# Planning TensorE's order together with the other engines in a two-layer hybrid attention trunk

## The chip, the cores and the metric

The kernel runs on one core of one Trainium2 chip. A core has a matrix engine (TensorE, PE in the profile, its weight loads PEld), a vector engine (VectorE, DVE), a scalar engine (ScalarE, ACT), a general engine (GpSimd, POOL) and a sync engine (SyncE, SP), which here only issues transfers (DMAs). Each engine works through its own list of instructions in order and waits at semaphores where one of them needs what another engine makes. The metric is device time in microseconds (us) of one execution; lower is better.

## The reference

The input `x` is 1024 tokens by 1024 features, in float32. Two layers follow each other, each `x + W_out(mixer(RMSNorm(x)) * silu(gate))`, with 16 heads of 64.

```python
def fox_mixer(h, w_in, b_f, q_g, k_g):          # layer 1
    proj = h @ w_in                              # q, k, v, gate (1024 each), 16 forget logits
    q = rms_norm(q, q_g); k = rms_norm(k, k_g)   # per head
    c = cumsum(log_sigmoid(f_logit + b_f), axis=1)
    o = softmax(q k^T / 8 + c_q - c_k, causal) v # in blocks of 128 queries
    return o, gate

def dsw_mixer(h, cos, sin, w_in, q_g, k_g):     # layer 2
    proj = h @ w_in                              # 3 groups of q, k, v (9216) and gate (1024)
    for g, (window, dilation) in enumerate(((128, 1), (512, 4), (2048, 16))):
        o[g], lse[g] = dilated_window_attention(rotary(rms_norm(q[g])), rotary(rms_norm(k[g])), v[g], window, dilation)
    return softmax(lse over g) * o summed over g, gate
```

## The kernel before, in words

**Tiling.** The 1024 tokens are eight tiles of 128, the 1024 features eight slices of 128. Float32 operands of the large products are split into a high and a low float16 half: `xh`, `xl` for the activations, `w[:, 0]`, `w[:, 1]` for the weights. `project` (line 678, matmuls on line 683) makes one token tile times up to 384 columns in 8 x 3 = 24 matmuls (high by high, high by low, low by high for each slice) into one bank of PSUM, the accumulator memory, called `pj`. The pool `ps_pj` has three such banks, `ps_s` three for scores and small things (tag `s`), `ps_o` two for attention outputs (tag `o`).

**Stages.** `gates(0, ...)` projects the gate of layer 1 in three parts of columns; during its first part each token tile is normalised and split just ahead of its projection: `x_ready` calls `row_factor` (ACT and DVE make the tile's factor `dg`), `spread_factor` (line 933, two small matmuls into `nb`) and `split_xt` (lines 964 to 967, DVE, ACT, POOL). Eight blocks of two heads (`hp`) of forgetting attention follow: eight projections each, `heads_tile` and `heads_pair` (norms, a float16 pair `hl`), a transposing DMA into `qk_t` (line 823), `scores` (line 843, tile `s`), the exponentials, a transposing DMA into `ptt` (line 891) and the products with the values, `pv` (lines 898 to 900, tile `o`). Results go to `y_d` in DRAM and come back through `turn_y` and `transpose_rows` (line 717, tile `pt`); those of the last head pair through `turn_last`. The output projection is `project_t` (line 707) in three parts; `grown`, `factors` (line 1219, tile `so`) and `take` normalise and split for layer 2 (`xl` on line 1236). Layer 2 has the same gates, then 24 blocks (eight head pairs by three dilations, `dsw_pair`, outputs `ob`), and its own `project_t`.

**Weights.** A block of weights is loaded two blocks ahead into `raw`. `bound` (lines 617 to 623) takes its norms into `vm`, `scale` (`spread_sums`, line 590, a small matmul `ws` or into the spare columns of a running `pj`) makes a power of two, `split` (lines 648 to 653) the two halves. These calls are spread by a slot clock, `Flow`: `project` and `project_t` tick it, 32 ticks a block, and `flow.at(slot, fn)` puts work into the source at a later tick. `scale` of the next block is at tick 8.

**What sets the order.** Source order is what the Python loops and `Flow` give. TensorE keeps it: `manual_schedule` pins it (lines 423 and 424). The order of the other four engines is written out by a planner. `step_graph` finds what each instruction must follow, `latest_starts` when it is due, `plan_engines` (line 294) plays the program through with a duration for each instruction (`lasts`) and lists the others' instructions by due time among those ready, with 150 ns of slack (`SLACK`) on each hand-over between engines. `order_engines` then ties each engine's list together. In that play TensorE takes `pe[at]`, the next in source order, and waits for it. A DMA on SP is held until the last TensorE instruction ahead of it in the source has begun.

Of the kernel before, what the change touches and what calls it, by code (L numbers as in the profile page):

```python
# [103 lines left out]


BYTES = {"float32": 4, "float16": 2, "bfloat16": 2, "int32": 4, "float32r": 4}
OTHERS = ("DVE", "Activation", "Pool", "SP")
OVERLAP = {"PE": 0, "DVE": 80, "Activation": 95, "Pool": 42}
SIGNAL = {"PE": 70, "DVE": 33, "Activation": 40, "Pool": 80, "SP": 27}
DRAIN = 200  # L110
SLACK = 150


class Access:
# [160 lines left out]
def latest_starts(steps, deps, need):  # L275


    n, t = len(steps), 0.0
    late = [0.0] * n
    for k, x in enumerate(steps):  # L280
        late[k] = t if x.eng == "PE" else t + 30000.0
        t += x.ns if x.eng == "PE" else 0.0
    for k in range(n - 1, -1, -1):
        e = steps[k].eng
        for d in deps[k] | need[k]:
            x = steps[d]
            if x.eng == "PE":
                continue
            took = 1900 + x.moved() / x.rate() if x.eng == "SP" else x.ns
            late[d] = min(late[d], late[k] - took - (SIGNAL[e] if x.eng != e else 0))  # L290
    return late


def plan_engines(steps, deps, need, after, slots):


    n = len(steps)
    late = latest_starts(steps, deps, need)
    succ, starts, fills = [[] for _ in range(n)], [[] for _ in range(n)], [[] for _ in range(n)]
    left = [len(d) for d in deps]  # L300
    for k in range(n):
        for d in deps[k]:
            succ[d].append(k)
    for a, b in set(after):
        if steps[a].eng != "PE":
            starts[a].append(b)
            left[b] += 1
    for bufs, rows in slots:
        queue = [f for f, _ in rows[bufs:]][::-1]
        for f in queue:  # L310
            left[f] += 1
        for _, us in rows:
            slot = [len(us), 0.0, queue]
            for u in us:
                fills[u].append(slot)
    pe = [k for k in range(n) if steps[k].eng == "PE"]
    gate, c = [], -1
    for x in steps:
        c += x.eng == "PE"
        gate.append(c)  # L320
    ready, end, begun = [0.0] * n, [0.0] * n, [-1.0] * len(pe)
    held, pe_ready = {}, set()
    soon, now = ({e: [] for e in OTHERS} for _ in range(2))
    free = dict.fromkeys(("PE",) + OTHERS, 0.0)
    out = {e: [] for e in OTHERS}
    pool_end = lock_end = dma_end = 0.0
    at = 0

    def open_up(k):
        left[k] -= 1  # L330
        if left[k]:
            return
        e = steps[k].eng
        if e == "PE":
            pe_ready.add(k)
        elif e == "SP" and gate[k] >= 0 and begun[gate[k]] < 0:
            held.setdefault(gate[k], []).append(k)
        else:
            if e == "SP" and gate[k] >= 0:
                ready[k] = max(ready[k], begun[gate[k]])  # L340
            heapq.heappush(soon[e], (ready[k], late[k], k))

    for k in range(n):
        left[k] += 1
        open_up(k)
    for _ in range(n):
        best = None
        for e in free:
            if e == "PE":
                if at == len(pe) or pe[at] not in pe_ready:  # L350
                    continue
                t = max(free[e], ready[pe[at]])
            elif now[e]:
                t = free[e]
            elif soon[e]:
                t = max(free[e], soon[e][0][0])
            else:
                continue
            if best is None or t < best[0]:
                best = (t, e)  # L360
        t, e = best
        if e == "PE":
            k, begun[at] = pe[at], t
            for j in held.pop(at, ()):
                ready[j] = max(ready[j], t)
                heapq.heappush(soon["SP"], (ready[j], late[j], j))
            at += 1
        else:
            while soon[e] and soon[e][0][0] <= t:
                _, p, k = heapq.heappop(soon[e])  # L370
                heapq.heappush(now[e], (p, k))
            k = heapq.heappop(now[e])[1]
            out[e].append(steps[k].ins)
        x, s = steps[k], t
        if e == "SP":
            dma_end = max(dma_end, t + 400) + x.moved() / x.rate()
            free[e], end[k] = t + x.ns, dma_end + 1500
        else:
            if x.lock:
                s = max(t, pool_end - 190)  # L380
                lock_end = s + x.ns
            elif e == "Pool":
                s = max(t, lock_end - 150)
                pool_end = s + x.ns
            end[k] = s + x.ns
            free[e] = end[k] - OVERLAP[e]
        tail = DRAIN if e == "PE" else 0
        for slot in fills[k]:
            slot[0] -= 1
            slot[1] = max(slot[1], end[k] + tail)  # L390
            if not slot[0] and slot[2]:
                j = slot[2].pop()
                ready[j] = max(ready[j], slot[1] + SIGNAL[steps[j].eng] + SLACK)
                open_up(j)
        for j in starts[k]:
            ready[j] = max(ready[j], t)
            open_up(j)
        for j in succ[k]:
            q = steps[j].eng
            if q != e:  # L400
                ready[j] = max(ready[j], end[k] + tail + SIGNAL[q] + SLACK)
            elif e not in ("PE", "SP"):
                ready[j] = max(ready[j], end[k])
            elif e == "SP":
                ready[j] = max(ready[j], end[k] + SIGNAL[q] + SLACK)
            open_up(j)
    return out
# [12 lines left out]
@with_exitstack  # L420
def trunk(ctx, tc, ins, out, cfg):
    nc = tc.nc
    if cfg["pin"]:
        ctx.enter_context(tc.manual_schedule(engines={mybir.EngineType.PE}))
    x, pos = ins["x"], ins["pos"]
    norm_g, gains, b_f = ins["norm_g"], ins["gains"], ins["b_f"]
    w_fox, w_dsw = ins["w_fox"], ins["w_dsw"]
# [425 lines left out]
    def v_tile(t2):  # L853
        vt = lay([P, NT, 2, 129], F16, name="vt", tag="vt")
        nc.scalar.activation(vt[:, :, :, 128], t2.unsqueeze(2).broadcast_to([P, NT, 2]), AF.Copy, scale=VS)
        return vt
# [79 lines left out]
    def column_factor(t):  # L936

        sq = lay([P, D], F32, name="xsq", tag="ptt")
        nb = ps_s.tile([P, 512], F32, name="nb", tag="s")
        for h in range(2):  # L940
            nc.scalar.activation(sq[:, 512 * h : 512 * (h + 1)], xts[t, h], AF.Square)
            for k in range(4 * h, 4 * h + 4):
                nc.tensor.matmul(nb[:, :P], ones.bitcast(F32), sq[:, k * P : (k + 1) * P], start=(k == 0), stop=(k == KT - 1))
        v, a, y = (nb[:, i * P : (i + 1) * P] for i in (1, 2, 3))
        r = sm.tile([P, P], F32, name="dg", tag="dg", bufs=2)
        nc.vector.tensor_scalar(v, nb[:, :P], 1.0 / D, EPS, ALU.mult, ALU.add)
        nc.scalar.activation(r, v, AF.Ln)
        nc.scalar.activation(r, r, AF.Exp, scale=-0.5)
        nc.scalar.activation(a, r, AF.Square)
        c = sm.tile([P, P], F32, name="cf", tag="dg", bufs=2)  # L950
        nc.vector.tensor_copy(c, v)
        nc.vector.scalar_tensor_tensor(a, a, -0.5, c, ALU.mult, ALU.mult)
        nc.vector.scalar_tensor_tensor(y, a, 1.5, r, ALU.add, ALU.mult)
        return y
# [23 lines left out]
    nb = column_factor(0)  # L978
# [9 lines left out]
    nb = column_factor(1)  # L988
# [165 lines left out]
    for hp in range(NHP):  # L1154
# [11 lines left out]
        vt = v_tile(w.t2)  # L1166
        for t in range(NT):
            ps = project(w, tile_cols(0, t))
# [12 lines left out]
            if hp == NHP - 1:  # L1181

                a = max(flow.now + 1, s0 + cfg["due"][t] - 4 * NT + cfg["lpf"] + 9)
# [210 lines left out]
    for ci, (hp, g) in enumerate(order):  # L1394
# [5 lines left out]
        vt = v_tile(w.t2)  # L1400
        qks = [None]
        for t in range(NT):
            if ci == NHP - 1:
                reload_x(t)
            ps = project(w, tile_cols(g, t))
# [19 lines left out]
            else:  # L1425
                cmb = {}
# [30 lines left out]
    layer["cm"].__exit__(None, None, None)  # L1457


CFG = dict(pin=1, bc=((1, 0, 26), (1, 1, 28), (0, 0, 38), (0, 1, 46)), wpool=3, rbufs=8, ps=0, pv=100, ph_=100, ph=1, wbufs=8, pl=3, um=3, lpf=8, lsd=((16, 16), (16, 14), (14, 11)), ty2=((0, 4), (1, 5)), hb=2, ub=2, qb=1, nb=3, fox=(((0, 0, 2, 2), (2, 4)), ((0, 0), (4, 4))), due=(29, 33, 39, 45, 35, 41, 49, 57), l1=dict(ga=7, ptt=4, ph=3, p=4, qk_t=6, vt=3, gsl=3), l2=dict(ga=4, cmb=3, ptt=3, ph=3, p=2, qk_t=3, og=3, vt=3, gsl=3, par=1), wload=(18, 20, 22, 24), wbound=(0, 1, 3, 4), wscale=8, wsplit=(10, 16, 22, 12))  # L1460


def host_layout(inputs):
# [49 lines left out]
```

## Time and profile before

| | us |
|---|---|
| runs | 1745.38, 1737.65, 1745.68 |
| median | 1745.38 |
| the profiled execution, its own time | 1739.07 |
| its span, first to last instruction | 1737.3 |
| TensorE busy | 1628.6 |
| VectorE busy | 1244.4 |
| ScalarE busy | 1076.8 |
| GpSimd busy | 858.4 |

The profile is of one execution. Busy time is the union of an engine's instructions; TensorE's ends are modelled, so that its busy time is not time at its peak. A wait is idle time of an engine just before an instruction, put down to what released it last. The clock is the share of full speed that TensorE was granted. DMA share is the mean busy share of the core's 16 DMA engines.

### The profile page before, as it was taken

How to read it: one execution, taken by the hardware profiler on the slowest of the kernel's cores; microseconds unless marked ns; L12 is line 12 of the kernel's file. 1: busy time of each engine (PE TensorE's matmuls, PEld its weight loads, DVE VectorE, ACT ScalarE, POOL GpSimd, SP SyncE). 2: the span in 40 equal slices, each digit the busy share in tenths (PEclk: the TensorE clock that was granted, in tenths of full speed). 3: DMA queues.
4: the chain of work that ended last, by engine and by line, in shares of the span. 5: the costliest groups of instructions: out<-in, count | busy, mean ns of one | idle time of the engine just before them, and what ended most of it. 6: DMA issues, size and time to landing. Idle time of an engine off the chain costs nothing.

```text
span 1737.3 us, 37952 instructions
## 1 busy us (share of the span) xinstructions
PE 1628.6 (94%) x13342; PEld 1052.0 (61%) x13342; DVE 1244.4 (72%) x3906; ACT 1076.8 (62%) x2790; POOL 858.4 (49%) x1019
## 2 busy tenths in 40 slices
PE   5799999999989687999999999999999999999999
PEld 3465666666656333666666666666666666666544
DVE  6686777776767538767767788777877778778751
ACT  5564767767767346656666677666666666666630
POOL 3211556555555233115555556566665766657420
PEclk9899999999999899999999999999999999999999
DMA  6334899999998768425877899887678777978852
GB/s 206 106 121 110 191 199 192 198 198 204 211 190 198 195 187 245 125 94 125 161 158 137 156 186 194 167 173 157 149 180 168 172 156 155 193 156 163 192 174 103
DMA packets 658767, 292.86 MB, mean 169 GB/s; under 512 B 510208, under 2 KB 622848, under 8 KB 658576
## 3 DMA queue, kind: packets, MB, share of 16 engines
q1 hardware_dynamic: 658576, 290.44, 74.0%
q8 instruction: 104, 1.70, 0.4%
q14 instruction: 87, 0.71, 0.1%
HBM read 124.35 MB, written 41.22 MB: 95 GB/s over the span
## 4 chain that ended last, share of the span: by engine, by line
PE 76%; DVE 9%; DMA 8%; issue 3%; ACT 2%; SPq 1%; POOL 1%; DVEq 0%; ACTq 0%; POOLq 0%
PE pj L683 58%; PE pj L707 6%; PE s L843 6%; DMA qk_t<-hl 3%; DVE w L649 1%; DVE p L1083 1%; DMA raw<-in_w_fox 1%; DMA ptt<-ph 1%; PE ob L900 1%; PE ob L898 1%; PE ob L899 1%; DMA yt<-y_d 1%; PE pt L717 1%; DVE hl L819 1%; PE o L900 1%
## 5 line engine op out<-in xcount | busy, mean ns | idle before, releaser
L683 PE MATMUL pj<-w,xh 128*128 128x384 f16 (+2 forms) x4864 | 1179.9, 326 | 0.5 <-DVE vt L782 0.3
L683 PE MATMUL pj<-w,xl 128*128 128x384 f16 (+2 forms) x2432 | 792.7, 326 | 11.9 <-DVE xl L1236 11.9
L683 PEld LDWEIGHTS <-xh 128*128 128x128 f16 x4864 | 470.8, 99 | 281.1 <-issue 10.6
L683 PEld LDWEIGHTS <-xl 128*128 128x128 f16 x2432 | 239.8, 99 | 168.5 <-DVE xl L1236 14.4
L890 POOL TENSOR_TENSOR ph<-p,ph 128x512 f16<-128x512 f32 (+3 forms) x176 | 170.7, 990 | 162.8 <-issue 91.0
L1314 POOL TENSOR_TENSOR ph<-p,ph 128x768 f16<-128x768 f32 (+2 forms) x96 | 155.0, 1615 | 117.2 <-ACT ph L1313 112.1
L818 POOL TENSOR_TENSOR hl<-u,hl 128x512 f16<-128x512 f32 x128 | 158.2, 1236 | 90.3 <-ACT hl L817 89.4
L649 DVE SCALAR_TENSOR_TENSOR w<-raw,ws_f,w 128x768 f16<-128x768 f32 (+2 forms) x133 | 170.3, 1285 | 7.2 <-ACT w L648 6.7
L843 PE MATMUL s<-qk_t 128*128 128x128 f16 (+1 forms) x1504 | 159.2, 247 | 17.1 <-DMA qk_t<-hl 17.1
L707 PE MATMUL pj<-xh,w 128*128 128x512 f16 x512 | 160.5, 383 | 1.5 <-DVE xr L1198 1.5
L771 DVE TENSOR_TENSOR u<-pj,gr 128x256 f32<-128x256 f32 x256 | 107.3, 419 | 68.3 <-PE pj L683 66.1
L884 ACT ACTIVATE p<-p,acc 128x512 f32<-128x512 f32 (+2 forms) x192 | 110.6, 608 | 72.8 <-DVE acc L1083 69.1
L776 ACT ACTIVATE sq<-pj 128x256 f32<-128x256 f32 x256 | 96.6, 377 | 86.7 <-DVE u L771 85.0
L843 PEld LDWEIGHTS <-qk_t 128*128 128x128 f16 x1504 | 113.1, 98 | 31.4 <-DMA qk_t<-hl 18.9
L648 ACT ACTIVATE w<-raw,ws_f 128x768 f16<-128x768 f32 (+2 forms) x133 | 119.1, 912 | 15.5 <-DVE ws_f L631 11.7
L1309 ACT ACTIVATE p<-p,og 128x128 f32<-128x128 f32 (+1 forms) x256 | 105.1, 441 | 36.7 <-DVE og L1308 36.3
L707 PEld LDWEIGHTS <-w 128*128 128x128 f16 x768 | 74.6, 99 | 85.3 <-issue 5.3
L898 PEld LDWEIGHTS <-ptt 128*128 128x128 f16 x1136 | 106.1, 98 | 23.6 <-DMA ptt<-ph 11.7
L803 POOL TENSOR_TENSOR ra<-u,cs 128x128 f32<-128x128 f32 x96 | 44.8, 466 | 138.0 <-DVE u L771 135.2
L899 PEld LDWEIGHTS <-ptt 128*128 128x128 f16 x1136 | 105.5, 97 | 11.7
L651 POOL TENSOR_SCALAR raw<-raw,ws_f 128x768 f32<-128x768 f32 (+2 forms) x43 | 38.7, 900 | 149.1 <-DVE ws_f L634 53.7
L617 ACT ACTIVATE jk<-raw 128x768 f16<-128x768 f32 (+2 forms) x88 | 72.2, 820 | 60.0 <-DMA raw<-in_w_dsw 32.1
(212 smaller groups left out, 2911.3 us busy)
## 6 DMA issues: line engine op xcount, KB each, us to landing
raw<-in_w_dsw SPq DMA_DIRECT2D x96, 384.0 KB, 4.1
raw<-in_w_fox SPq DMA_DIRECT2D x32, 384.0 KB, 3.8
og_d<-og SPq DMA_DIRECT2D x64, 132.0 KB, 2.8
cmb<-og_d SPq DMA_DIRECT2D x64, 132.0 KB, 3.1
bc<-c_d SPq DMA_DIRECT2D x32, 256.0 KB, 3.8
gs_d<-ge SPq DMA_DIRECT2D x32, 192.0 KB, 2.1
xt<-in_xt SPq DMA_DIRECT2D x16, 256.0 KB, 4.6
gsf<-gs_d SPq DMA_DIRECT2D x64, 64.0 KB, 2.6
```

Source lines behind the costliest of these rows:

```text
L648: nc.scalar.activation(w[:, 0, :, :n], raw, AF.Copy, scale=self.sw)
L649: nc.vector.scalar_tensor_tensor(w[:, 1, :, :n], raw, self.sw, w[:, 0, :, :n], ALU.mult, ALU.subtract)
L683: nc.tensor.matmul(ps[:, :n], a[:, k, cols], w.slab(k, j), start=(k == 0 and i == 0), stop=(k == KT - 1 and i == 2))
L707: nc.tensor.matmul(ps[m], w.slab(k, j)[:, m * P : (m + 1) * P], a[:, k, 512 * b : 512 * (b + 1)], start=(k == 0 and x == 0), stop=(k == KT ...
L771: nc.vector.tensor_mul(u[:, t % 2].rearrange("p (a b) d -> p a b d", a=2), ps[:, : 4 * HD].rearrange("p (a b d) -> p a b d", a=2, b=2), gr ...
L818: nc.gpsimd.tensor_sub(hl[:, :, :4, 1], u, hl[:, :, :4, 0])
L843: nc.tensor.matmul(s[:, c0 : c0 + cnt * P].rearrange("p (c s) -> p c s", c=cnt), qk[:, i, blk], kk[:, j : j + cnt, e], start=(h == 0), sto ...
L884: nc.scalar.activation(p, p, AF.Exp, bias=acc, scale=-1.0)
L890: (nc.gpsimd if pool_l else nc.vector).tensor_sub(ph[:, e, 1, cols], p, ph[:, e, 0, cols])
L898: nc.tensor.matmul(o[:, e, :], hi, vt[:, j, e, HD:], start=(b == 0), stop=False, skip_group_check=True)
L899: nc.tensor.matmul(o[:, e, :HD], hi, vt[:, j, e, :HD], start=False, stop=False, skip_group_check=True)
L1314: nc.gpsimd.tensor_sub(ph[:, 1], st["p"], ph[:, 0])
```

## The change

TensorE is no longer pinned. In the planner it becomes an engine like the others: its instructions wait in `soon` until they are ready and then in `now`, from which the first in source order is taken, where the others take the one that is due first. A hand-over to TensorE carries a slack of 400 ns (`PE_SLACK`) where the others keep 150. The tiles of one tag (a bank of PSUM among them) still begin in source order, which now is an edge of the graph for TensorE too. A DMA on SP is held until as many TensorE instructions have been issued as stand ahead of it in the source. The list made for TensorE is tied together like the others'. No instruction is added, removed or altered.

```diff
-OTHERS = ("DVE", "Activation", "Pool", "SP")
+ENGINES = ("PE", "DVE", "Activation", "Pool", "SP")
+PE_SLACK = 400
...
     for a, b in set(after):
-        if steps[a].eng != "PE":
-            starts[a].append(b)
-            left[b] += 1
+        starts[a].append(b)
+        left[b] += 1
...
+    margin = {e: PE_SLACK if e == "PE" else SLACK for e in ENGINES}
...
-        if e == "PE":
-            pe_ready.add(k)
-        elif e == "SP" and gate[k] >= 0 and begun[gate[k]] < 0:
+        if e == "SP" and gate[k] > len(out["PE"]):
             held.setdefault(gate[k], []).append(k)
         else:
-            if e == "SP" and gate[k] >= 0:
-                ready[k] = max(ready[k], begun[gate[k]])
-            heapq.heappush(soon[e], (ready[k], late[k], k))
+            heapq.heappush(soon[e], (ready[k], k if e == "PE" else late[k], k))
...
-            if e == "PE":
-                if at == len(pe) or pe[at] not in pe_ready:
-                    continue
-                t = max(free[e], ready[pe[at]])
-            elif now[e]:
+            if now[e]:
                 t = free[e]
...
+        while soon[e] and soon[e][0][0] <= t:
+            _, p, k = heapq.heappop(soon[e])
+            heapq.heappush(now[e], (p, k))
+        k = heapq.heappop(now[e])[1]
+        out[e].append(steps[k].ins)
         if e == "PE":
-            k, begun[at] = pe[at], t
-            for j in held.pop(at, ()):
-                ready[j] = max(ready[j], t)
-                heapq.heappush(soon["SP"], (ready[j], late[j], j))
-            at += 1
-        else:
-            while soon[e] and soon[e][0][0] <= t:
-                _, p, k = heapq.heappop(soon[e])
-                heapq.heappush(now[e], (p, k))
-            k = heapq.heappop(now[e])[1]
-            out[e].append(steps[k].ins)
+            for j in held.pop(len(out[e]), ()):
+                heapq.heappush(soon["SP"], (max(ready[j], t), late[j], j))
...
             if q != e:
-                ready[j] = max(ready[j], end[k] + tail + SIGNAL[q] + SLACK)
+                ready[j] = max(ready[j], end[k] + tail + SIGNAL[q] + margin[q])
...
-    if cfg["pin"]:
-        ctx.enter_context(tc.manual_schedule(engines={mybir.EngineType.PE}))
```

More of the change, by code (lines that the diff above doesn't have):

```diff
@@ L315, in plan_engines @@
                 fills[u].append(slot)
-    pe = [k for k in range(n) if steps[k].eng == "PE"]
-    gate, c = [], -1
+    gate, c = [], 0
     for x in steps:
+        gate.append(c)
         c += x.eng == "PE"
[L320 to L325, printed above, removed]
+    ready, end = [0.0] * n, [0.0] * n
+    held = {}
+    soon, now = ({e: [] for e in ENGINES} for _ in range(2))
+    free = dict.fromkeys(ENGINES, 0.0)
+    out = {e: [] for e in ENGINES}
     pool_end = lock_end = dma_end = 0.0
-    at = 0
+    margin = {e: PE_SLACK if e == "PE" else SLACK for e in ENGINES}
     def open_up(k):
@@ L347, in plan_engines @@
         best = None
-        for e in free:
-            if e == "PE":
-                if at == len(pe) or pe[at] not in pe_ready:
-                    continue
-                t = max(free[e], ready[pe[at]])
-            elif now[e]:
+        for e in ENGINES:
+            if now[e]:
                 t = free[e]
@@ L392, in plan_engines @@
                 j = slot[2].pop()
-                ready[j] = max(ready[j], slot[1] + SIGNAL[steps[j].eng] + SLACK)
+                ready[j] = max(ready[j], slot[1] + SIGNAL[steps[j].eng] + margin[steps[j].eng])
                 open_up(j)
@@ L1457, in trunk @@
     layer["cm"].__exit__(None, None, None)
-CFG = dict(pin=1, bc=((1, 0, 26), (1, 1, 28), (0, 0, 38), (0, 1, 46)), wpool=3, rbufs=8, ps=0, pv=100, ph_=100, ph=1, wbufs=8, pl=3, um=3, lpf=8, lsd=((16, 16), (16, 14), (14, 11)), ty2=((0, 4), (1, 5)), hb=2, ub=2, qb=1, nb=3, fox=(((0, 0, 2, 2), (2, 4)), ((0, 0), (4, 4))), due=(29, 33, 39, 45, 35, 41, 49, 57), l1=dict(ga=7, ptt=4, ph=3, p=4, qk_t=6, vt=3, gsl=3), l2=dict(ga=4, cmb=3, ptt=3, ph=3, p=2, qk_t=3, og=3, vt=3, gsl=3, par=1), wload=(18, 20, 22, 24), wbound=(0, 1, 3, 4), wscale=8, wsplit=(10, 16, 22, 12))
+CFG = dict(bc=((1, 0, 26), (1, 1, 28), (0, 0, 38), (0, 1, 46)), wpool=3, rbufs=8, ps=0, pv=100, ph_=100, ph=1, wbufs=8, pl=3, um=3, lpf=8, lsd=((16, 16), (16, 14), (14, 11)), ty2=((0, 4), (1, 5)), hb=2, ub=2, qb=1, nb=3, fox=(((0, 0, 2, 2), (2, 4)), ((0, 0), (4, 4))), due=(29, 33, 39, 45, 35, 41, 49, 57), l1=dict(ga=7, ptt=4, ph=3, p=4, qk_t=6, vt=3, gsl=3), l2=dict(ga=4, cmb=3, ptt=3, ph=3, p=2, qk_t=3, og=3, vt=3, gsl=3, par=1), wload=(18, 20, 22, 24), wbound=(0, 1, 3, 4), wscale=8, wsplit=(10, 16, 22, 12))
 def host_layout(inputs):
```

## The prediction

> **What bounds the kernel now.** I read the page's busy line, its chain, then busy time by stage, and last TensorE's waits.
>
> ```profile
> span 1737.3 us, 37952 instructions
> PE 1628.6 (94%) x13342; PEld 1052.0 (61%) x13342; DVE 1244.4 (72%) x3906; ACT 1076.8 (62%) x2790; POOL 858.4 (49%) x1019
> PE 76%; DVE 9%; DMA 8%; issue 3%; ACT 2%; SPq 1%; POOL 1%; DVEq 0%; ACTq 0%; POOLq 0%
> ```
>
> TensorE (PE) is busy 94% of the span and 76% of the chain that ended last. 1737.3 - 1628.6 leaves 109 us in which it waits. The next view cuts the span into stages: first gate block (0:80), the rest of that layer's gates (80:160), forgetting attention (160:500), its end with the start of the output projection (500:590), that projection (590:640), passage to layer two (640:700), dilated attention (700:1600), end (two rows). Columns: stretch and length, busy us and count of PE, weight loads, DVE, ACT, POOL, then granted clock, DMA share, GB/s.
>
> ```profile
> 0.00:80.00 80.00, 48.66 (x257) 30.88 (x258) 55.58 (x128) 44.88 (x100) 28.08 (x33) 0.89 0.48 163
> 80.00:160.00 80.00, 77.63 (x533) 51.82 (x532) 59.89 (x168) 41.87 (x98) 10.64 (x8) 1.00 0.35 103
> 160.00:500.00 340.00, 321.09 (x3318) 226.15 (x3317) 248.25 (x853) 240.21 (x609) 192.24 (x187) 0.98 0.94 196
> 500.00:590.00 90.00, 75.05 (x772) 50.67 (x769) 55.00 (x166) 53.67 (x120) 38.27 (x37) 0.94 0.92 214
> 590.00:640.00 50.00, 37.31 (x168) 16.66 (x167) 24.39 (x67) 21.88 (x40) 12.12 (x10) 0.86 0.45 137
> 640.00:700.00 60.00, 45.26 (x222) 21.91 (x220) 49.02 (x58) 37.36 (x51) 19.77 (x14) 0.92 0.82 244
> 700.00:1600.00 900.00, 896.74 (x7307) 585.65 (x7306) 683.99 (x2281) 588.55 (x1659) 521.26 (x686) 1.00 0.75 159
> 1600.00:1680.00 80.00, 73.45 (x533) 44.20 (x532) 54.08 (x166) 44.97 (x113) 33.45 (x43) 0.98 0.79 190
> 1680.00:1738.00 58.00, 53.41 (x249) 24.08 (x246) 14.22 (x24) 3.43 (x4) 2.55 (x2) 1.00 0.30 105
> ```
>
> The long dilated stage has 900 - 896.7 = 3.3 us of idle PE: no order can win there. The idle time lies before 700 (31.3, 2.4, 18.9, 15.0, 12.7, 14.7) and at the end (6.6, 4.6). What PE waited for, with total, times and longest:
>
> ```profile
> PE nb L933 <- DVE dg L928: 19.3, 5, 7.2
> PE s L843 <- DMA qk_t<-hl: 17.1, 11, 2.6
> PE pg L738 <- DVE gm L736: 13.1, 2, 11.7
> PE ws L590 <- ACT vm L623: 12.7, 1, 12.7
> PE pj L683 <- DVE xl L1236: 11.9, 5, 4.3
> PE pt L717 <- DMA yt<-y_d: 11.0, 6, 6.3
> PE o L898 <- DMA ptt<-ph: 8.2, 7, 3.3
> ```
>
> Except for pg (the first matmul of all), each is a small matmul at the head of PE's pinned queue, with projection matmuls behind it. The question for each is whether those are ready then, and whether the waiting chain ends the stage anyway.
>
> **The change part by part.** It adds and removes no instruction, only reorders. The rule "first in source order among those ready" can only pass over a matmul that the planner believes late. Projections may run ahead within the three `pj` banks, since the first writers of a tag's tiles stay in source order. What is passed over stays queued with what needs it: behind nb the splitting of one token tile, behind ws the weights of the next part, behind s and o the rest of one attention tile. The other engines and SP's queue are planned again around the new PE times. A DMA on SP was released once one certain matmul had begun; now it is once as many matmuls have been issued as stand ahead of it. Run-ahead of two tiles (2 x 3.91 us, row below) thus frees loads at most 7.8 us earlier; they still need their buffers, and I cost this at nothing. If it pulls loads in front of transposes, it is part of the given-back case below. Terms are gains against the profiled execution, 1739.07 us (span 1737.3 and 1.8 around it).
>
> *First gate block (nb).* Rows of PE, POOL and the chain (start, us, what):
>
> ```profile
> 50.81 0.77 PE L933 MATMUL nb<-dg,ones 128*128 128x128 f32 x2 [7.15 <-DVE dg L928]
> 39.31 1.53 POOL L967 TENSOR_TENSOR xl<-xt,xh 128x512 f16<-128x512 f32 x1 [1.21 <-ACT xh L966]
> 44.64 1.59 POOL L967 TENSOR_TENSOR xl<-xt,xh 128x512 f16<-128x512 f32 x1 [1.81 <-DVE ge L870]
> 67.38 1.15 POOL L967 TENSOR_TENSOR xl<-xt,xh 128x512 f16<-128x512 f32 x1 [4.49 <-ACT xh L966]
> 51.58 5.69 PE pj L683 x24
> 57.49 3.91 PE pj L683 x24
> 64.96 13.40 PE pj L683 x72
> ```
>
> PE stands 7.15 us before nb at 50.81, while the next two token tiles are complete at 40.8 and 46.2: two projections of 3.91 us fit. After the wait, 24 matmuls take 5.69 us instead of 3.91: the clock costs 1.8 more. But the last token tile is only split at 68.5, by DVE, ACT and POOL. Its projection can end at 68.5 + 3.9 = 72.4, where now the last three end at 78.4: at most 6 us stay, 2 more if the DVE chain starts earlier. If gate work on DVE and ACT, now earlier, delays that chain, 0. I take 5 (0 to 8). The 2.4 us of 80:160 I leave.
>
> *Forgetting attention (s and o).* Idle is 18.9 us, but the DMA share is 0.94: 340 x 0.94 = 320 us of transfers, so at a share of 1.00 the stage cannot lose more than 20. Two bounds agree; on top, each s waits on a transpose whose own latency stays:
>
> ```profile
> 420.02 4.42 DMA qk_t<-hl
> 425.26 1.95 PE pj L683 x12
> 474.19 0.72 PE L843 MATMUL s<-qk_t 128*128 128x256 f16 x6 [1.91 <-DMA qk_t<-hl]
> 474.97 3.63 PE pj L683 x12
> ```
>
> Nearer the end where DMA allows little, since the queue holds 94% already: 6 (0 to 19). The last two rows show the clock again: after a wait of 1.91 us twelve matmuls took 3.63 us instead of 1.95. The Trainium skill, "TensorE: Matmul & The Clock Gate" (Part 1), has the clock halved after an idle window of about 3.4 us that runs free of the kernel. The row shows it after a shorter wait, so the row decides. By the page only waits above 3.4 us would repay those 1.8 us, by the row shorter ones can too; the sum has no term of its own for the clock.
>
> *End of attention (pt, o).* The longest pt wait, 6.3 us, can be filled with the last head pair's projections, three tiles of 3.91. What follows is a chain, however (scores, exponentials, transposes at a DMA share of 0.92, then the last `turn_last`), and the projection's accumulations hold all three banks until it is done. Idle moved forward reappears before that. I take 4 (0 to 13, of 15.0 idle).
>
> *Output projection (ws).* Rows of PE, ACT, DVE, and the chain:
>
> ```profile
> 611.45 0.37 PE L590 MATMUL ws<-vm,ones 128*128 128x4 f32 x1 [12.69 <-ACT vm L623]
> 604.73 0.36 ACT L553 ACTIVATE sn<-rt 128x192 f32<-128x192 f32 x1 [5.21 <-DVE rt L543]
> 611.22 0.18 ACT L623 CAST vm<-vm 128x2 fp32r<-128x2 f32 x1
> 615.70 1.67 DVE L649 SCALAR_TENSOR_TENSOR w<-raw,ws_f,w 128x768 f16<-128x768 f32 x1 [0.72 <-ACT w L648]
> 611.82 24.25 PE pj L707 x105
> ```
>
> The largest single term. PE stops from 598.8 to 611.45 for `ws`, the weight norm of part 3, because ACT sits in the sine table's work until 605 and makes `vm` at 611.2. But `scale` is called at tick 8 of 32 of part 2, which has 2 column tiles x 2 halves x 8 x 3 = 96 matmuls: 72 are left, at 24.25 / 105 = 0.231 us each 16.6 us, ready behind it. They cover the 12.7. Part 2 would end at 615, where part 3's weights are being split (615.7 + 1.7 = 617.4): perhaps 2 us of waiting come back there. I take 10; 5 if outputs parked in the banks wait for ACT's late work, 13 with the clock (0.86 here): 5 to 13.
>
> *Passage to layer two (xl, so).* `project` waits in k order for single xl slices:
>
> ```profile
> 667.95 0.34 PE L683 MATMUL pj<-w,xl 128*128 128x384 f16 x1 [2.64 <-DVE xl L1236]
> 673.44 0.50 PE L683 MATMUL pj<-w,xl 128*128 128x384 f16 x1 [4.34 <-DVE xl L1236]
> ```
>
> Meanwhile the same k of the next two token tiles is there, so up to two tiles can be part-filled: 2.64 + 4.34 and as much again in the second half. But DVE is busy 49 of 60 us and must also empty the three banks, which then finish together. 5 (0 to 12).
>
> *Dilated stage.* 0. Gain at most 3.3; a loss is bounded by one wait per weight block of the kind in the row below, 24 x 0.48 = 12: -12 to 3. *End*: pt waits before work that is ready, then a final projection that cannot be shortened: 3 (0 to 7).
>
> ```profile
> 864.06 0.83 PE L843 MATMUL s<-qk_t 128*128 128x128 f16 x8 [0.48 <-DMA qk_t<-hl]
> PE s L843 <- DMA qk_t<-hl: 3.0, 3, 1.5
> ```
>
> Sum: 5 + 6 + 4 + 10 + 5 + 0 + 3 = 33; 1739.07 - 33 = 1706. Of the runs shown two lie 6.5 us above the profiled one and one 1.4 below it; I add 3, and forecast **1709**. All upper ends together give 75 (1664), all lower ends a loss of 7 (1746).
>
> **The rivals.**
>
> *Given back by banks and DMA.* Everything run ahead ends in a full `pj` bank or the transposes' queue, and only `ws`, whose cover lies in the same part, stays: 10 us, 1732. For: DMA 0.94, DVE 49 of 60. Against: DMA 0.45 in 590:640. The Trainium skill's "Perfetto Trace Analysis" (Optimization Strategy) says that bubbles which repeat on the saturated engine can mean that PSUM lacks room for the next tile; here the row names a transpose instead (s waits for `qk_t`).
>
> *Nothing moves.* The plan's durations put every operand in time, and PE's order comes out as it was: 1745. Against: the plan's own ready times carry a slack of 400 ns for PE, so it sees waits before they happen.
>
> *Slower, decided in the dilated stage.* PE has no slack there, and a matmul that the plan moves ahead of projections which it believes late (weights being split) must be ready in truth. The stage has 24 blocks x 4 tile pairs = 96 score groups behind a transpose; the last row above (waits in 700:1600) prices a missed one at 3.0 / 3 = 1.0 us. It decides from 33 misses on; at every second pair, 48 us: 1757. Against: the plan passes only what it thinks late, and it has nearly nothing late here.
>
> *All waits filled.* Upper ends nearly throughout: 1675.
>
> **How the numbers follow.** Likeliest case 0.50 (its own range 1692 to 1726); given back 0.14, of which 0.04 lands within half a per cent; nothing moves 0.10; slower 0.14; all filled 0.12. About 0.5% (8.7 us) is what a measurement of this kernel tells from no change. Faster 0.50 + 0.10 + 0.12 = 0.72, same 0.04 + 0.10 = 0.14, slower 0.14. Range 1668 to 1744: it leaves out the slower case and a little of the fastest.
>
> **What would show it.** Right: the `ws` wait gone or under 3 us, with PE busy 590 to 640 above 45; nb waits under 8 in total; s waits under 8; the dilated stage still under 5 us idle. Wrong: the same totals under other names (pj waiting for bank emptying, o or pt longer), DMA share at 1.00 with the forgetting stage as long as now, or new s and ob waits after 700.

## The result

The changed kernel takes 1687.33 us (median; 1684.16 to 1689.63), the kernel before beside it 1741.52 (1737.35 to 1745.68): a ratio of 0.9688, 95% interval 0.9652 to 0.9724, 54 us less. The forecast was 1709 with a range of 1668 to 1744. Faster was right and the range holds the time, but the gain is 54 us where the sum of the forecast's terms was 33, and the likeliest case's own range (1692 to 1726) ends 5 us above it.

The page of the changed kernel, its span, busy time and chain (profiled execution 1684.16 us; its lines of code are numbered 15 lower than before):

```profile
span 1682.4 us, 37953 instructions
PE 1623.1 (96%) x13342; PEld 1048.6 (62%) x13342; DVE 1234.0 (73%) x3906; ACT 1080.0 (64%) x2790; POOL 858.8 (51%) x1019
PE 80%; DMA 9%; DVE 6%; ACT 2%; issue 2%; SPq 1%; POOL 0%; DVEq 0%; ACTq 0%; POOLq 0%
```

The same 13342 matmuls. Idle PE fell from 108.7 to 59.3 us, 49.4 less, and their busy time by 5.5, from 1628.6 to 1623.1: together the 54.9 by which the span is shorter. The second part is the clock (0.980 before, 0.991 now): matmuls run slower for a while after some waits, and there are fewer waits.

Stages now end earlier, so fixed windows of the two traces no longer hold the same work. The boundaries below are ends of the same matmul, counted in each trace: the end of layer 1's gates; of the seventh attention block's projections; the last `o` of the attention; the last matmul of the output projection; the end of part 1 of layer 2's gates; the last `ob` of the dilated attention; the end. Busy time by stage, columns as in the prediction; before:

```profile
0.00:135.30 135.30, 102.19 (x640) 68.22 (x641) 99.09 (x248) 76.78 (x170) 33.42 (x37) 0.94 0.42 141
135.30:468.10 332.80, 315.74 (x3185) 219.92 (x3184) 241.23 (x822) 226.99 (x581) 178.28 (x172) 0.99 0.90 189
468.10:586.30 118.20, 100.80 (x1038) 69.81 (x1037) 77.76 (x242) 76.87 (x175) 57.53 (x57) 0.95 0.95 209
586.30:664.00 77.70, 62.21 (x277) 27.65 (x275) 40.11 (x87) 34.51 (x58) 19.65 (x15) 0.90 0.60 182
664.00:713.30 49.30, 37.36 (x198) 20.11 (x196) 43.72 (x63) 33.54 (x52) 14.33 (x12) 0.86 0.65 198
713.30:1672.30 959.00, 950.93 (x7740) 619.50 (x7738) 724.77 (x2415) 621.81 (x1745) 552.62 (x726) 1.00 0.76 162
1672.30:1733.40 61.10, 59.36 (x277) 26.83 (x274) 16.98 (x32) 6.32 (x12) 2.55 (x2) 1.00 0.33 117
```

and changed:

```profile
0.00:122.70 122.70, 100.80 (x639) 66.88 (x640) 97.19 (x247) 76.44 (x170) 34.93 (x37) 1.00 0.47 155
122.70:434.60 311.90, 310.51 (x3186) 218.77 (x3184) 235.41 (x823) 230.02 (x581) 173.90 (x172) 1.00 0.96 202
434.60:548.20 113.60, 103.53 (x1058) 70.64 (x1056) 76.68 (x242) 77.07 (x174) 59.10 (x57) 0.98 0.99 220
548.20:609.00 60.80, 58.04 (x255) 25.16 (x254) 37.79 (x85) 31.18 (x57) 18.01 (x13) 0.95 0.72 215
609.00:659.90 50.90, 40.34 (x197) 20.59 (x198) 45.04 (x65) 37.23 (x53) 16.18 (x13) 0.83 0.70 206
659.90:1615.60 955.70, 948.87 (x7739) 619.16 (x7738) 724.37 (x2415) 622.62 (x1747) 553.80 (x726) 1.00 0.77 163
1615.60:1678.70 63.10, 61.01 (x277) 27.37 (x274) 16.77 (x31) 5.39 (x10) 2.89 (x2) 0.97 0.30 105
```

The forecast's windows lay near these stages but were not the same.

| stage | before, us | changed, us | gain | of it idle PE | forecast (its bounds) |
|---|---|---|---|---|---|
| gates of layer 1 | 135.3 | 122.7 | 12.6 | 11.2 | 5 (0 to 8) |
| attention, blocks 0 to 6 | 332.8 | 311.9 | 20.9 | 15.7 | 6 (0 to 19) |
| block 7 and the last `o` | 118.2 | 113.6 | 4.6 | 7.3 | 4 (0 to 13) |
| output projection | 77.7 | 60.8 | 16.9 | 12.7 | 10 (5 to 13) |
| passage to layer two | 49.3 | 50.9 | -1.6 | 1.4 | 5 (0 to 12) |
| gates 2, dilated attention | 959.0 | 955.7 | 3.3 | 1.2 | 0 (-12 to 3) |
| end | 61.1 | 63.1 | -2.0 | -0.4 | 3 (0 to 7) |

Idle is the stretch less PE's busy time. The gains add up to 54.7. In the two stages around the last `o`, some 20 matmuls of the output projection have moved from the later into the earlier one (277 to 255, 1038 to 1058): with their 4.2 us (62.21 - 58.04) put back, block 7 gains about 9 and the output projection 12.7. One trace's stages scatter by several us in the attention: experiments below with edits elsewhere ended their last `o` at 552.0 (`a_rot`) and 557.0 (`pin_rest`), where the changed kernel did at 548.2. In the six traces that leave the attention free at the same slack and banks (the changed kernel, `a_rot`, `pin_gates`, `pin_out`, `pin_rest`, `due`), block 7 and the last `o` take 113.6 to 118.3 us; the changed kernel's is the shortest, and before it was 118.2.

What TensorE waited for in the changed kernel:

```profile
PE pg L723 <- DVE gm L721: 12.1, 1, 12.1
PE pj L668 <- DVE xl L1221: 7.8, 6, 2.1
PE o L883 <- DMA ptt<-ph: 5.8, 3, 2.7
PE s L828 <- DMA qk_t<-hl: 4.4, 6, 1.3
PE pj L668 <- ACT xh L951: 4.2, 4, 2.2
PE pj L692 <- DVE xr L1434: 3.8, 2, 2.1
PE nb L918 <- DVE nv L910: 3.7, 2, 2.5
PE pt L702 <- DMA yt<-y_d: 3.6, 4, 2.1
```

`nb` went from 19.3 to 3.7, `s` from 17.1 to 4.4, `pt` from 11.0 to 3.6, `ws` from 12.7 to nothing. In the first gates 4.2 us of waiting for `xh` (line 951) came in place of some of `nb`. The first wait, `pg`, has no ready work behind it and stays.

That the matmuls behind were let past can be counted in the two traces, by the large matmuls (`project` and `project_t`) begun ahead of each small one. Ahead of the `ws` that waited 12.7 us there are 58 more of them than before, ahead of the `pt` that waited 6.3 us 33 more, ahead of the five waiting `nb` 10 to 32 more, and ahead of the eight `s` of the first attention that waited over half a us 10 to 18 more. The `ws` now stands between two matmuls of the projection, without a wait:

```profile
571.73 0.27 PE L575 MATMUL ws<-vm,ones 128*128 128x4 f32 x1
571.87 0.39 PE L692 MATMUL pj<-xl,w 128*128 128x512 f16 x1
```

### The profile page after: what moved, and what is told of

Same layout as the page of the kernel before. It is cut to its first block, busy times and chain, and to the rows that moved or that the text cites. A ratio compares the mean times of both kernels' runs of the same rounds, so it can differ in the third digit from the quotient of the medians.

```text
span 1682.4 us, 37953 instructions
## 1 busy us (share of the span) xinstructions
PE 1623.1 (96%) x13342; PEld 1048.6 (62%) x13342; DVE 1234.0 (73%) x3906; ACT 1080.0 (64%) x2790; POOL 858.8 (51%) x1019
## 4 chain that ended last, share of the span: by engine, by line
PE 80%; DMA 9%; DVE 6%; ACT 2%; issue 2%; SPq 1%; POOL 0%; DVEq 0%; ACTq 0%; POOLq 0%
PE pj L668 61%; PE s L828 7%; PE pj L692 6%; DMA qk_t<-hl 3%; DMA ptt<-ph 1%; PE ob L885 1%; PE ob L883 1%; PE ob L884 1%; DMA yt<-y_d 1%; PE o L885 1%; PE o L883 1%; PE o L884 1%; DVE w L634 1%; DMA xr<-in_xp 1%; PE pt L702 1%
## 5 line engine op out<-in xcount | busy, mean ns | idle before, releaser
L668 PEld LDWEIGHTS <-xl 128*128 128x128 f16 x2432 | 238.6, 98 | 164.3 <-DVE xl L1221 11.2
L875 POOL TENSOR_TENSOR ph<-p,ph 128x512 f16<-128x512 f32 (+3 forms) x176 | 171.2, 995 | 137.2 <-issue 77.7
L1299 POOL TENSOR_TENSOR ph<-p,ph 128x768 f16<-128x768 f32 (+2 forms) x96 | 154.7, 1612 | 124.4 <-ACT ph L1298 120.1
L883 PEld LDWEIGHTS <-ptt 128*128 128x128 f16 x1136 | 106.1, 98 | 18.4 <-DMA ptt<-ph 7.4
L884 PEld LDWEIGHTS <-ptt 128*128 128x128 f16 x1136 | 105.5, 97 | 11.5
L636 POOL TENSOR_SCALAR raw<-raw,ws_f 128x768 f32<-128x768 f32 (+2 forms) x43 | 39.4, 917 | 141.3 <-DVE ws_f L619 100.5
L885 PEld LDWEIGHTS <-ptt 128*128 128x128 f16 x1136 | 105.7, 97 | 0.0
```

What stands on the lines that cost most here:

```text
L668: nc.tensor.matmul(ps[:, :n], a[:, k, cols], w.slab(k, j), start=(k == 0 and i == 0), stop=(k == KT - 1 and i == 2))
L875: (nc.gpsimd if pool_l else nc.vector).tensor_sub(ph[:, e, 1, cols], p, ph[:, e, 0, cols])
L883: nc.tensor.matmul(o[:, e, :], hi, vt[:, j, e, HD:], start=(b == 0), stop=False, skip_group_check=True)
L884: nc.tensor.matmul(o[:, e, :HD], hi, vt[:, j, e, :HD], start=False, stop=False, skip_group_check=True)
L885: nc.tensor.matmul(o[:, e, :], lo, vt[:, j, e, HD:], start=False, stop=(b == n - 1), skip_group_check=True)
L1299: nc.gpsimd.tensor_sub(ph[:, 1], st["p"], ph[:, 0])
```

## Experiments

### Undoing the change stage by stage

The changed kernel with TensorE's steps pinned to source order in one stretch of the program and free elsewhere. The edges are given to the planner's graph, so the other engines are planned around the pinned order, as they were before.

```diff
-def order_engines(tc, rows):
+def order_engines(tc, rows, lo, hi):
...
+    deps, need, after, slots = step_graph(steps, rows)
+    held = [k for k, (at, _) in enumerate(own) if lo <= at < hi and steps[k].eng == "PE"]
+    after.extend(zip(held, held[1:]))
```

`pin_gates` holds layer 1's gates, `pin_fox` the eight attention blocks, `pin_out` the output projection and what the source has between it and layer 2's gates, `pin_rest` all from those gates on, with the projections of the passage; `pin_all` holds every TensorE step (`held` without the bounds).

> The changed kernel, with TensorE held to source order in the first layer's gate blocks alone (0 to 123 us of it). Theory (each stage's gain is made by passing over that stage's own waits, and the gains add): the 12.5 us by which the end of the gates came earlier are given back, 1697 to 1700 against the changed kernel's 1687, and the later stages keep their lengths. Rival (the gain comes from the other engines' new plan, which the order of TensorE only sets off): within 5 us of 1687.

> The changed kernel, with TensorE held to source order in the forgetting attention's eight blocks alone. Theory (own waits, additive): 21 us of the seven first blocks and some 3 at the end come back, 1708 to 1715. Rival (the stage is bound by transfers, whose share was 0.94 and is 1.02 now, and it got shorter because the queue is fed differently): within 8 us of 1687.

> The changed kernel, with TensorE held to source order in the first output projection and the passage to layer two. Theory: the wait for the weight norm behind the sine table (12.7 us) and its slow clock return, 1699 to 1704, and the passage itself does not change (its gain was -0.5). Rival (the wait would not return, since what ScalarE does is planned otherwise now): within 5 us of 1687.

> The changed kernel, with TensorE held to source order from the second layer's gates to the end. Theory (nothing late there before): 1685 to 1692, at most 3 us of the dilated stage come back. Rival (the end gains, as I had forecast with 3 us, or the dilated stage depends on the new order by now): 1693 or more.

> The changed kernel with all of TensorE's steps kept in source order by edges of the graph; what is left of the change is the new slack of 400 ns towards TensorE and the new condition that holds a DMA on SP (as many TensorE instructions issued as stand ahead of it). Theory (the whole gain is TensorE's order): 1742 us, 1736 to 1748, with the ws wait of 12 us, the nb and s waits of 17 to 19 us each back. Rival (part of the gain comes from SP's transfers being freed by a count or from the longer slack): at most 1734, with s waits under 13 us in total.

| pinned | median, us | ratio to before (95%) | longer than the changed kernel |
|---|---|---|---|
| nothing (the changed kernel) | 1687.33 | 0.9688 (0.9652 to 0.9724) | |
| gates 1 | 1699.81 | 0.976 (0.9737 to 0.9782) | 12.5 |
| attention | 1711.16 | 0.9835 (0.9813 to 0.9858) | 23.8 |
| output projection | 1704.02 | 0.9788 (0.977 to 0.9807) | 16.7 |
| layer 2 | 1694.41 | 0.972 (0.9686 to 0.9754) | 7.1 |
| everything | 1745.22 | 1.0025 (1.0013 to 1.0038) | 57.9 |

The first three came out as expected, `pin_out` at the upper edge. The four single stretches cost 60.1 together, all at once 57.9: to within the scatter, the gains of the stages add, and what one stage is ahead the next neither needs nor returns. The waits of `nb`, `s` and `ws` each come back at about their old length when their own stretch is held, and not when another is. TensorE's waits, in part, with the gates pinned, with the attention pinned, with the output projection pinned, and with all pinned:

```profile
PE nb L922 <- DVE dg L917: 17.2, 5, 7.7
```
```profile
PE s L832 <- DMA qk_t<-hl: 18.2, 13, 2.7
...
PE pt L706 <- DMA yt<-y_d: 8.0, 3, 7.0
```
```profile
PE ws L579 <- ACT vm L612: 12.6, 1, 12.6
```
```profile
PE nb L921 <- DVE dg L916: 16.8, 5, 7.2
PE s L831 <- DMA qk_t<-hl: 15.8, 11, 3.3
...
PE ws L578 <- ACT vm L611: 12.6, 1, 12.6
```

`pin_all` also settles what the slack of 400 ns towards TensorE does without the new order: it is worth nothing, and the kernel takes about 4 us longer than before (0.13 to 0.38%). On the new condition for SP's transfers it can say little, since with TensorE in source order as many matmuls have been issued as stand ahead of a transfer just when the last of these has begun, which is the old condition. So the rival of `pin_all` falls as far as the slack goes; a run with the new order and the old condition wasn't made. Against freed transfers as the main cause stands the count above: at the waits of before, the large matmuls really went first, and in `pin_all` the same count is unchanged.

`pin_rest` missed my expectation (1685 to 1692): its time lies in the rival's range. Its trace, though, is already 10.1 us behind the changed kernel's where the pinned stretch begins (619.1 against 609.0 at the last matmul of the output projection) and 12.1 at the end, so the pinned stretch accounts for about 2 us; the table's stages of layer 2 also give 3.3 - 2.0 = 1.3. The rest of that trace's delay arose where nothing was pinned, and what caused it stays open.

### Taking the largest wait away without the new order

Before, ACT works on the sine table while `ws` needs it. Here `rotary_tables` is called 16 ticks later, behind `scale`, in the kernel before (`b_rot`) and in the changed one (`a_rot`).

```diff
         if h == 1:
-            rotary_tables()
+            flow.at(flow.now + 16, rotary_tables)
```

> The kernel before (TensorE pinned), with the rotary tables' work put 16 ticks later in the second part of the output projection, behind the weight norm's matmul. Theory (ScalarE's sine work alone makes that 12.7 us wait, and with it most of the projection's gain): the wait is under 4 us and the kernel takes 10 to 16 us off its 1742, 1726 to 1732. Rival (transfers or the weights make the norm late anyway): within 5 us of 1742.

> The changed kernel with the same move of the rotary tables' work. Theory (its TensorE passes over that wait already): within 4 us of 1687. Rival (the weight norm still sets when part three can begin): 5 to 10 us faster.

`b_rot`: 1736.22 us (0.9969, 0.9952 to 0.9986), 5 to 6 less than before. That is less than the 10 to 16 I expected and about the rival's bound of 5, and this although the wait of 12.7 is gone and the projection's first 240 matmuls end 14.6 us earlier. `a_rot`: 1688.47 (0.9691, 0.9666 to 0.9716), as the changed kernel. Where `b_rot` gives it back: TensorE's waits of `b_rot` from 575 to 720, in part, then the stretch from matmul 240 of the output projection to its last, in `b_rot` and before:

```profile
PE pj L707 <- ACT w L648: 5.7, 1, 5.7
PE so L1219 <- DVE sacc L1211: 4.4, 2, 3.0
```
```profile
614.40:660.30 45.90, 37.17 (x149) 15.38 (x147) 27.66 (x49) 24.57 (x40) 13.43 (x10) 0.85 0.68 200
```
```profile
629.00:664.00 35.00, 32.20 (x148) 14.49 (x147) 17.78 (x28) 16.07 (x24) 11.30 (x9) 1.00 0.76 223
```

The stretch is 10.9 us longer for the same matmuls: 5.9 more idle (8.7 against 2.8), of which part 3's weights being split account for 5.7 in a new wait of `w`, and 5.0 more busy time, at a clock of 0.85 where it was 1.00. So in the pinned order more than half of the wait came back further down the queue. In the changed kernel matmuls that are ready stand in for it, and the gain stays.

### Is the run-ahead of the projections all of it?

`proj`: the projections' matmuls (`pj`) keep source order among themselves, and the small ones may still be passed over, as in the changed kernel.

```diff
+    held = [k for k, x in enumerate(steps) if x.eng == "PE" and x.outs[0].name.startswith("pj")]
+    after.extend(zip(held, held[1:]))
```

> The changed kernel, with the projections' matmuls held in source order among themselves, and all the others (nb, ws, s, o, pt) free around them. Theory (what is passed over is one small matmul at a time, and the next projection behind it is the work that fills): attention and output projection keep their gains, the part-filled tiles of the first gate block and of the passage are lost, 1688 to 1696. Rival (part-filling several banks is where the gain is): 1700 or more.

1691.46 us (0.9703, 0.9667 to 0.9739): 4 more than the changed kernel, with intervals that overlap. Attention and end of attention keep their gain. The `xl` wait is back at its length of before, and from matmul 240 of the output projection to the end of part 1 of gates 2 the trace of `proj` is 6.2 us longer than the changed kernel's (the wait, then the stretch in `proj` and in the changed kernel):

```profile
PE pj L671 <- DVE xl L1224: 12.0, 5, 4.3
...
578.60:669.60 91.00, 74.11 (x345) 35.38 (x345) 63.77 (x95) 55.68 (x84) 30.19 (x23) 0.89 0.68 203
```
```profile
575.10:659.90 84.80, 72.93 (x344) 34.93 (x345) 64.19 (x94) 55.41 (x84) 28.97 (x22) 0.90 0.73 218
```

About 50 of the 54 us thus come from passing over small matmuls, with the projections kept in their order. Filling several banks in parts is worth at most a few us, not clear of the scatter. It is not the passage that shows them, in spite of the `xl` wait: 5.5 of the 6.2 us lie before the last matmul of the output projection (39.4 against 33.9), and the passage itself is 0.7 longer.

### The slack

`PE_SLACK` says how late the planner believes an operand to come to TensorE. 1500 and 150 in place of 400:

```diff
-PE_SLACK = 400
+PE_SLACK = 1500   # slack150: 150
```

> The changed kernel with 1500 ns of slack for TensorE instead of 400. Theory (TensorE has projections to fill with, so lateness of an attention matmul costs little, while true landing times scatter by more than 400 ns): the same or up to 5 us faster, 1682 to 1689. Rival (each put-off lengthens the chain through transposes that bounds the end of attention and the passage): 1692 or more.

> The changed kernel with PE_SLACK 150, as the other engines have, in place of 400. Theory (from the run with 1500: the longer the slack, the more small matmuls are put off, and the end of attention, a chain, pays for it; below 400 little is left to gain there): 1685 (1680 to 1691), the last o within 3 us of the changed kernel's, waits for s and o a few us more in total. Rival (the slack is what saves PE from waiting for operands that come later than planned): s, o and pt waits 10 us more in total and 1694 or more.

1500: 1703.02 us (0.9773, 0.9754 to 0.9793), 16 more. Through the seventh block it loses 5, but from there to the last `o` it takes 124.4 where the changed kernel took 113.6. 150: 1686.12 (0.9682, 0.9666 to 0.9698), no difference from 400. The waits of `o` for `ptt` come to 14.8 us with 1500 and 15.0 with 150, where the changed kernel has 5.8; so it is not these waits that set the time.

With 1500 the rival was right against my theory. The score matmuls of the attention's end (those that ran from 470 us on in the kernel before) come behind 34 more large matmuls than before on average, with 400 behind 14. That fits the rival's reason: this end is a chain through scores, exponentials, transposes and `o`, and a matmul of the chain which is put off lengthens it. With 150 the time came out as expected, its trace less so: the last `o` is 6.7 us later than the changed kernel's (554.9 against 548.2), not within 3, which is inside the scatter of that point (up to 557.0 in `pin_rest`), and the `o` waits are 9 us longer. Which of 150 and 400 is better these runs don't tell; nothing speaks for more than 400.

### A fourth bank

Four banks for projections and two for scores and small things:

```diff
-    ps_pj = pool("ps_pj", 3, PSUM)
-    ps_s = pool("ps_s", 3, PSUM)
+    ps_pj = pool("ps_pj", 4, PSUM)
+    ps_s = pool("ps_s", 2, PSUM)
```

> The changed kernel with four banks for projections and two for scores and small things in place of three and three. Theory (what the new order passes over is one small matmul at a time, and one or two tiles of run-ahead cover it): the fourth bank gives nothing, 1687 (1680 to 1692), or costs where a score tile waits for one of two banks (s or nb waiting on ACT or DVE, up to 1700). Rival (the run-ahead ends in full banks, as the prediction's given-back case had it): gates and the eight attention blocks 5 to 15 us shorter, 1672 to 1682.

1680.42 us (0.9637, 0.9615 to 0.966), the shortest time of all, though its interval still touches the changed kernel's, and it lies in both expected ranges. Stages of its trace (blocks 0 to 6; block 7 and the last `o`; from the end of part 1 of gates 2 to the end), the same last stretch of the changed kernel below:

```profile
116.80:434.00 317.20, 312.09 (x3185) 218.60 (x3183) 247.87 (x823) 229.35 (x583) 181.20 (x173) 1.00 0.98 199
434.00:558.90 124.90, 112.58 (x1083) 75.05 (x1080) 75.60 (x242) 76.50 (x172) 56.63 (x56) 0.95 0.98 199
...
666.70:1675.70 1009.00, 1007.17 (x8014) 645.70 (x8012) 739.23 (x2450) 632.10 (x1759) 576.03 (x728) 1.00 0.75 161
```
```profile
659.90:1678.70 1018.80, 1009.88 (x8014) 646.53 (x8012) 741.14 (x2446) 628.02 (x1757) 556.69 (x728) 1.00 0.74 159
```

In the attention the fourth bank gives nothing, and the end of the attention is 11.3 us longer; 25 more matmuls of the output projection run in it, but the projection behind it is no shorter for that (61.6 against 60.8). So far my theory held: blocks 0 to 6 have only 1.4 us of idle time with three banks, and at the end a score tile now waits for one of its two banks to be emptied, which was named as the cost:

```profile
PE s L828 <- DVE xl L708: 3.4, 2, 2.3
```

As one bank was taken from the scores for it, these runs can't tell what a fourth bank alone would do there. But the theory fell in layer 2. There the idle time goes from 8.9 us to 1.8. The wait of `s` from the end of part 1 of gates 2 on, changed kernel first:

```profile
PE s L828 <- DMA qk_t<-hl: 4.0, 5, 1.3
```
```profile
PE s L828 <- DMA qk_t<-hl: 1.1, 2, 0.5
```

The wait for a bank that the last residual adds had to empty (`xr`, 3.8 us in the changed kernel's waits above) is gone, and `s` is down to 1.1. `pj4` also starts better: SP's new order puts the load that the first wait hangs on ahead of the weights (issued at 1.66 us, not at 4.46), and that wait, 12.1 us in the changed kernel, is 4.8:

```profile
PE pg L723 <- DVE gm L721: 4.8, 1, 4.8
```

Three and three banks in layer 1 with four and two in layer 2 might take both gains; that wasn't tried.

### Due times through TensorE

The other engines work by due times, and `latest_starts` doesn't carry these backwards through TensorE's steps: what feeds only a small matmul isn't seen as urgent. `due` carries them through.

```diff
-            if x.eng == "PE":
-                continue
-            took = 1900 + x.moved() / x.rate() if x.eng == "SP" else x.ns
+            took = 1900 + x.moved() / x.rate() if x.eng == "SP" else x.ns + (DRAIN if x.eng == "PE" and e != "PE" else 0)
```

> The changed kernel, but the due times that order the other engines are also carried backwards through TensorE's steps, so that what feeds a small matmul (sacc before so, the emptying of the last banks before sacc) is due before what feeds only a later projection. Theory (the passage to layer two is set by a DVE chain whose last two residual adds are queued behind splits that are not needed yet): last matmul of the output projection to the end of part 1 of layer 2's gates shrinks from 50.9 us to 46 or less, and the kernel comes to 1682 (1677 to 1686). Rival (the transfers of x and of the split halves set that passage, or the earlier due times put DVE's other work out of order elsewhere): no change in the passage, 1687 or more; over 1693 if the orders of the attention are worse.

1683.73 us (0.967, 0.9649 to 0.9691): the changed kernel within the uncertainty. The passage stays (50.5 against 50.9 us), because DVE's order in it stays: the residual add that empties a last bank starts at 622.2, where it did at 621.6. So the time lies in my theory's range (1677 to 1686), but not for its reason: the passage stayed, as the rival had said, and what an earlier add would give stays open. The first wait is shorter again (7.2 for 12.1, its load issued at 2.13), but the first gates end only 1.2 us earlier for it; where the 3.6 us come from, if they are real, stays open.

## Why the prediction was right, and where its sizes were off

**The mechanism** was the one forecast: small matmuls at the head of PE's queue with ready projections behind them. Of what was named as signs, `ws` is gone, `nb` and `s` are under 8 us. PE's busy time in 590:640, which was to pass 45, reads 40.6 but means nothing any more, since that work now runs 38 to 55 us earlier; in the same stage idle went from 15.5 to 2.8. The dilated stage has 6.8 us idle with gates 2 included, 8.1 before; the window 700:1600 itself has 5.1, a hair above the 5 named, and also holds other work now.

**First gate block, 5 forecast, 10.8 measured, above the bound of 8.** Its end moved from 78.3 to 67.5. Two steps of that bound failed. The last token tile was taken to be split at 68.5; in the changed kernel POOL's last split is over at 65.5, since DVE's and ACT's work for it moved forward too:

```profile
64.30 1.16 POOL L952 TENSOR_TENSOR xl<-xt,xh 128x512 f16<-128x512 f32 x1 [3.25 <-ACT xh L951]
```

And its projection was taken to run for 3.9 us after the split; it ends at 67.5, 2.0 after, since the first of its 24 matmuls, on the slices that DVE had split before, were done by then. 3.0 and 1.9 are the 4.9 between the predicted best end, 72.4, and 67.5. The idle time of the other two parts, which the sum left out, gave 1.8 more, which makes the table's 12.6.

**Attention, 6 forecast, 20.9 measured.** This is the largest miss, and the step is "nearer the end where DMA allows little, since the queue holds 94% already". A share is no measure of what is left to gain: the stage moved the same bytes (332.8 us at 189 GB/s are 62.9 MB, 311.9 at 202 are 63.0), at a share of 0.96 for 0.90, and the next stage moved 220 GB/s at 0.99. Nor is 1.00 a ceiling: over 160:500 the changed kernel's trace reads 1.02. 0.94 was also the mean of a window that held part of block 7; the blocks themselves had 0.90. Idle PE in them fell from 17.1 to 1.4 us, so the transpose "whose own latency stays" was hidden too. The remaining 5.2 us are busy time of the same matmuls, 315.74 to 310.51: the prediction gave the clock no term. That no bound of DMA existed here is read from these rows; a run with more transfers wasn't made. The Trainium skill, "Perfetto Trace Analysis" (Identifying the Most-Contended Engine), warns of just this: with 16 DMA engines occupancy misleads, and HBM utilization, the rate as a share of its peak, is to be used instead. The trace agrees that the share misleads.

**End of attention, 4 forecast, 4.6 measured.** The reason was right: block 7's projections end 15.5 us further ahead than block 6's, and 10.9 of this are gone by the last `o`. That the size came so close is partly luck, since this stretch scatters by 4.7 us between traces with the same order rules (113.6 to 118.3).

**Output projection, 10 forecast, 12.7 without the moved matmuls.** `ws` itself was sized right. The 2 us that were to come back at part 3's weights didn't: idle is 2.8 in all. `b_rot` shows that this fear was the right one for a pinned order, with 5.7 us.

**Passage, 5 forecast, -1.6 measured.** Part-filling shortens the `xl` wait (7.8 us, 12.0 in `proj` without it), and idle fell by 1.4. But the matmuls themselves took 40.34 us for 37.36, at a clock of 0.83 for 0.86. DVE, busy 45.0 of 50.9 us, leads the chain of the passage; this is read from the trace, and `due`, which was to test it, left the order as it was. Up to 624 the residual adds stand in its order between splits, without a gap, and the norm for the second half waits for the last of them. The DVE timeline of the changed kernel:

```profile
619.39 2.38 DVE L1221 TENSOR_TENSOR xl<-xs,xh 128x512 f16<-128x512 f32 x1
621.58 0.71 DVE L1183 SCALAR_TENSOR_TENSOR xr<-pj,ws_f,xr 128x512 f32<-128x512 f32 x1
622.22 1.29 DVE L1221 TENSOR_TENSOR xl<-xs,xh 128x512 f16<-128x512 f32 x1
623.72 0.69 DVE L1196 TENSOR_TENSOR sacc<-sacc,nsq 128x512 f32<-128x512 f32 x1 [0.21 <-ACT nsq L1192]
```

The last output matmul is over at 609.0; its bank is read at 621.6. The warning beside that term, that DVE must also empty the banks, should have set it to nothing.

**Dilated stage and end, 3 forecast, 1.3 measured.** No loss from misses: `s` waits 4.0 us there. "No order can win there" holds for the order, but not for the banks (`pj4`).

**The rivals.** Given back by banks and DMA: true of the end of attention, and of `b_rot`, not of the rest. That repeating bubbles can mean a lack of room in PSUM (the Trainium skill, "Perfetto Trace Analysis", Optimization Strategy) did not fit the attention of layer 1, where a fourth bank gives nothing. In layer 2 the fourth bank took away 7 of the last 9 us of idle time. Nothing moves (1745) is what `pin_all` measures. Slower by misses in the dilated stage: there were none that count. All waits filled: the gates, the attention and the output projection came to their upper ends or above, the other stages not. The 3 us added for the median over the profiled run came out (1687.33 against 1684.16), which with four runs is partly luck.

## What to carry to other kernels

On an engine that works in order, read each wait together with what stands behind it: where ready work does, letting it pass keeps the time, while taking away the cause of one wait in a pinned order can hand much of it to the next (here 12.7 us gone, 5 to 6 kept). A high DMA share beside a waiting engine is not yet a bound: here the same bytes went through faster as soon as the engine ran on. Where a stage ends in a chain through a transpose or another engine's order, running ahead moves the wait and doesn't remove it.

## What the runs showed of the hardware

Of three waits of nearly the same length, two brought a stretch at half clock and the longest didn't. All three are of the kernel before, for the transpose into `qk_t`, with the six score matmuls behind each:

```profile
372.89 1.25 PE L843 MATMUL s<-qk_t 128*128 128x256 f16 x6 [2.15 <-DMA qk_t<-hl]
424.49 0.72 PE L843 MATMUL s<-qk_t 128*128 128x256 f16 x6 [2.62 <-DMA qk_t<-hl]
474.19 0.72 PE L843 MATMUL s<-qk_t 128*128 128x256 f16 x6 [1.91 <-DMA qk_t<-hl]
```

After 2.15 us the score matmuls themselves are slow (1.25 for 0.72); after 1.91 they are not, but the projections behind them are (3.63 us for twelve); after 2.62, the longest, neither is (1.95 for twelve). The granted clock in the two slow stretches:

```profile
372.52:375.93 3.41, 3.04 (x13) 1.81 (x14) 1.06 (x4) 1.06 (x2) 1.15 (x1) 0.50 0.98 218
474.92:478.33 3.41, 3.41 (x13) 1.64 (x11) 1.68 (x6) 2.04 (x6) 0.99 (x2) 0.50 0.83 162
```

Each lasts 3.41 us, one begins before the end of its wait and one 0.73 us after it, and their starts are 102.40 us apart, 30 times 3.413. The other slow stretches of this trace also last whole multiples of 3.41 us and begin on the same grid, and those of the changed kernel's trace do so on theirs. So the start of the slow stretch isn't tied to the wait's end, which agrees with a window that runs free of the kernel (the Trainium skill, "TensorE: Matmul & The Clock Gate", Part 1), but all three waits are shorter than the 3.4 us of idle time it names. For a kernel, the price of a wait is the wait and, depending on where it falls on that grid, a few us of half speed behind it. In the seven attention blocks, letting matmuls pass gained 15.7 us of waits and 5.2 of busy time.
